# The first projection unit as eight plain block products, with the split of S3 behind 60 of its 96 matmuls

## The chip, the core and the metric

The kernel runs on one core of one Trainium2 chip. The metric is the device time of one execution in microseconds (us); the figure that is compared is the median of several executions.

## What is computed

One layer of a bidirectional encoder over 2048 tokens of width 1024. Only its first line matters here, the combined input projection:

```python
u = x @ w_in
idx = np.cumsum(SPLIT_SIZES)[:-1].tolist()
q, k, v, a_gate, hy, h_gate, br_gate = jnp.split(u, idx, axis=-1)
```

`x` is 2048 x 1024 and `w_in` 1024 x 8704. What follows (windowed attention, a long convolution by FFT, gates, the output projection and a layer norm) is not touched by the change.

## The kernel before

**Tiling.** The projection is made transposed: 128 output columns (one tile of `w_in`) stand on the partitions, 512 tokens along the free axis. A unit (class `Unit`, L209) makes two such column tiles for two token chunks, so four 128x512 results, from a 2x2 scheme of blocks: the 1024 long inner dimension is cut into two halves of four 128-row pieces (k = 0 to 3), the tokens into two chunks, the columns into two tiles. Instead of eight block products it uses seven, M1 to M7, by the scheme of Strassen and Winograd: M1 and M2 take the raw blocks A11 and A12 of x, the others take sums S1 to S4 of blocks or A22 (table `XOP`, L34), and on the side of the weights the blocks B11 to B22 or their sums T1 to T4 (`WOP`, `TDEF`).

**Split in two.** Every operand is split in a high and a low part of reduced width: `split` (L55) makes the high part by a cast on ScalarE (ACT) and the low part by a subtraction on VectorE (DVE) or GpSimd (POOL). A block product is then 4 pieces x 3 matmuls (high x high, high x low, low x high; L274, L276, L278) = 12 matmuls of 128x512, a unit 84.

**Weights.** `Unit.load` brings two tiles of 512 KB into `w_raw` (three buffers, shared by all units). `Unit.prep` makes, for one product, the weight's sum on DVE (`w_tmp`, L227) and its split, high part on ACT, low part `w_l` on POOL. It runs four products ahead, in a ring of five buffers.

**The order of products.** `stream` (L242) strings the units' products together: M1 of a unit, then (of the unit before it) M4 and M3, then M2, M6, M5, M7, and so on. It is a Python generator: each `next` of it writes down one matmul. `finish` (L283) empties the results: `keep` copies a PSUM bank to SBUF on ACT (L286), `add` joins two of them on DVE (L293), M4 is copied on ACT (L307). A unit's sums Y, X and Z take the banks y0 and y1 (changing places from unit to unit) and zz; bank c is not used in this stage.

**The start, `hy_stage(0)` (L349).** The first unit is a `z_unit` (L385), the second a `g_unit` (L429), and so on by turns, 16 units. For the first one x is not yet there: `load_x` brings the blocks of token chunk 0 (`r0[k]`, A11 and A12 side by side, 512 KB each) and of chunk 1 (`r1[k]`, A21 and A22). They are kept in buffers that later hold other things: `raw` (L358) uses the three `u` buffers and the two `cv` buffers, and two of the `r1` tiles use `w_raw`. `r1[2]` thus waits until `r0[0]` is done with, and `r1[3]` until a weight tile of the first unit is. Then `split_x` splits A11 and A12 (low parts on DVE) and `sums_x` (L165) makes for each k the sums S1 to S4 into `xs` tiles on DVE (L168) and splits S2, S1 (DVE), S3, A22 and S4 (POOL). A `u` buffer is needed again as soon as the first result of a unit leaves PSUM (`new_u`, L363).

**What sets the order.** The engines work each through a queue in order. The order in the queues is not the order of the text: a planner at build time (a list scheduler with its own timing, priority by the order of the text) sets it, and a buffer goes to its next owner when all accesses to the earlier one are done. So a transfer written down far later, as the copies of `w_branch_attn` to `wa_d` (L462, in the second pass), can stand near the start.

**Lines that matter below.** L56 and L57 are the two halves of `split`, L163 the loads of x, L219 those of the weights, L227 the sums of weights, L168 the sums of x, L286 and L307 copies out of PSUM, L366 a memset at the head of a fresh `u` buffer.

## Time and profile before

| | us |
|---|---|
| median of 3 executions | 2641.27 |
| lowest to highest | 2640.31 to 2643.61 |
| the profiled execution, time | 2640.98 |
| the profiled execution, span on the core | 2639.2 |
| TensorE matmul (PE) busy | 2505.1 (95% of the span) |
| DVE busy | 1735.0 (66%) |
| ACT busy | 1520.2 (58%) |
| POOL busy | 1406.8 (53%) |

The span is the time from the first to the last instruction on the core. Times in the rows below are counted from its start. "Busy" includes time in which an instruction has started and stands still. An engine's idle time is put down to what ended it (`<-` and the releaser).

### The profile page before, as it was taken

The page shows a single profiled execution, that of the slowest core. Times are in us where ns is not written, and L with a number is a line of the kernel's source. Part 1 is how long each engine was busy: PE and PEld are TensorE (multiplying, and loading weights), DVE is VectorE, ACT ScalarE, POOL GpSimd, SP SyncE. Part 2 cuts the span into 40 slices and gives each one's busy share as a digit, 9 for nine tenths or more (in the row PEclk, how much of TensorE's full clock was granted, in tenths as well). Part 3 has the DMA queues.
Part 4 walks back from the last instruction along what each step waited for, and adds up shares of the span by engine and source line. Part 5 has one row for each costly group of instructions (what it writes and reads, how often), then busy time and mean ns, then how long its engine had stood idle before and what let it go on. Part 6 is the DMA issues. An engine that isn't in the chain of part 4 may idle for free. (4 is left out here: it accounts for less than half of the span.)

```text
span 2639.2 us, 39177 instructions
## 1 busy us (share of the span) xinstructions
PE 2505.1 (95%) x12364; PEld 2088.9 (79%) x12364; DVE 1735.0 (66%) x3323; ACT 1520.2 (58%) x2935; POOL 1406.8 (53%) x1410
## 2 busy tenths in 40 slices
PE   6999999999999999999999999998989988999998
PEld 4888877786788877888887888886778866888887
DVE  7866677657577775655541577777989924556555
ACT  4444444468688864445455678887666644334432
POOL 6655554475666655665545666667766634112220
PEclk8999999999999999999999999999999998999999
DMA  7733343544544544245668545446777668556662
GB/s 255 235 120 122 120 155 119 167 150 146 180 144 150 156 160 139 81 136 179 198 190 261 165 137 157 126 141 226 244 242 252 214 200 221 136 130 168 176 154 78
DMA packets 342788, 444.04 MB, mean 168 GB/s; under 512 B 133257, under 2 KB 214619, under 8 KB 341029
## 3 DMA queue, kind: packets, MB, share of 16 engines
q1 hardware_dynamic: 340965, 432.50, 53.2%
q0 software_dynamic: 1616, 9.04, 1.1%
q8 instruction: 98, 1.61, 0.3%
q14 instruction: 109, 0.89, 0.1%
HBM read 290.41 MB, written 168.08 MB: 174 GB/s over the span
## 5 line engine op out<-in xcount | busy, mean ns | idle before, releaser
L57 POOL TENSOR_TENSOR w_l<-w_tmp,w_h 128x512 fp32r<-128x512 f32 x272 | 371.7, 1368 | 291.0 <-ACT w_h L56 254.5
L57 POOL TENSOR_TENSOR w_l<-w_raw,w_h 128x512 fp32r<-128x512 f32 x204 | 298.4, 1465 | 143.8 <-ACT w_h L56 118.8
L56 ACT CAST w_h<-w_tmp 128x512 fp32r<-128x512 f32 x272 | 168.1, 619 | 212.8 <-PE ps_y L276 167.2
L56 ACT CAST w_h<-w_raw 128x512 fp32r<-128x512 f32 x204 | 126.5, 621 | 146.2 <-PE ps_zz L276 74.5
L943 POOL TENSOR_TENSOR xq<-xq 128x512 fp32r<-128x512 f32 x128 | 162.9, 1297 | 83.0 <-ACT xq L941 79.9
L789 ACT ACTIVATE pb<-pb,rm 128x385 f32<-128x385 f32 (+1 forms) x256 | 153.3, 601 | 71.6 <-DVE rm L786 62.7
L380 DVE SCALAR_TENSOR_TENSOR cv<-u,cw,cv 128x1024 f32<-128x1024 f32 (+1 forms) x96 | 142.0, 1479 | 69.3 <-ACT cv L377 69.1
L274 PE MATMUL ps_y<-xq,w_h 128*128 128x512 f32 x376 | 150.1, 399 | 6.4 <-ACT u L286 6.3
L278 PE MATMUL ps_y<-xq,w_l 128*128 128x512 f32 x376 | 147.6, 392 | 0.0
L276 PE MATMUL ps_y<-xq,w_h 128*128 128x512 f32 x376 | 147.2, 391 | 0.0
L1236 POOL TENSOR_TENSOR ar<-ar,ga 128x256 f32<-128x256 f32 x64 | 51.1, 801 | 173.6 <-ACT ga L1235 156.1
L783 DVE CUSTOM_DVE_ANT_0 pb<-ps_a,bias 128x384 f32<-128x384 f32 (+1 forms) x256 | 131.2, 534 | 17.7 <-PE ps_a L53 12.2
L57 DVE TENSOR_TENSOR pl<-ps_b,ph 128x512 fp32r<-128x512 f32 (+1 forms) x240 | 130.1, 561 | 13.3 <-ACT ph L56 11.4
L227 DVE TENSOR_TENSOR w_tmp<-w_raw,w_tmp 128x512 f32<-128x512 f32 x94 | 89.6, 953 | 69.5 <-POOL w_l L57 68.5
L227 DVE TENSOR_TENSOR w_tmp<-w_raw 128x512 f32<-128x512 f32 x94 | 98.1, 1044 | 56.2 <-DMA w_raw<-in_w_in_dram 37.7
L57 POOL TENSOR_TENSOR fl<-fl,fh 128x512 fp32r<-128x512 f32 x32 | 43.2, 1349 | 166.7 <-ACT fh L56 166.5
L53 PE MATMUL ps_y<-yh,b 128*128 128x256 f32 x688 | 130.0, 283 | 0.0
L286 ACT COPY u<-ps_y 128x512 f32<-128x512 f32 x204 | 119.0, 583 | 6.2 <-PE ps_y L278 5.9
L53 PE MATMUL ps_y<-xq,w_h 128*128 128x512 f32 x336 | 113.2, 407 | 3.5 <-ACT u L286 3.5
L53 PEld LDWEIGHTS ps_y<-yh,b 128*128 128x128 f32 x688 | 109.7, 191 | 1.7
L293 DVE TENSOR_TENSOR ev<-ps_zz,u 128x512 f32<-128x512 f32 x72 | 49.4, 686 | 93.7 <-ACT u L286 34.4
L53 PE MATMUL ps_c<-pl,v 128*128 128x256 f32 x368 | 99.4, 296 | 11.3 <-DVE pl L57 10.8
(370 smaller groups left out, 8325.3 us busy)
## 6 DMA issues: line engine op xcount, KB each, us to landing
w_raw<-in_w_in_dram SPq DMA_DIRECT2D x136, 512.0 KB, 3.7
xq<-zk_d SPq DMA_DIRECT2D x64, 512.0 KB, 4.9
br_d<-ev SPq DMA_DIRECT2D x64, 256.0 KB, 2.0
zk_d<-ko SPq DMA_DIRECT2D x64, 256.0 KB, 2.0
zk_d<-zo SPq DMA_DIRECT2D x64, 256.0 KB, 4.1
gc_d<-go SPq DMA_DIRECT2D x64, 256.0 KB, 2.5
fl<-gc_d SPq DMA_DIRECT2D x64, 256.0 KB, 5.0
ga<-br_d SPq DMA_DIRECT2D x64, 256.0 KB, 3.6
```

The source lines that it names most:

```text
L53: tc.keep_in_program_order(nc.tensor.matmul(*args, **kw))
L56: nc.scalar.copy(out=hi, in_=src)
L57: return (eng or nc.vector).tensor_tensor(out=lo, in0=src, in1=hi.bitcast(F32), op=ALU.subtract)
L227: w_sum[0].tensor_tensor(out=self.tmp[n], in0=i0, in1=i1, op=ALU.subtract)
L274: mmf(o, wh[:, k], xh[k], start=start and k == 0, stop=False, skip_group_check=not start)
L276: mmf(o, wh[:, k], xl[k], start=False, stop=False, skip_group_check=not start)
L278: mmf(o, wl[:, k], xh[k], start=False, stop=k == 3, skip_group_check=not start)
L286: nc.scalar.copy(out=u.tmp[n], in_=o)
L380: nc.vector.scalar_tensor_tensor(out=y[:, i0:hi], in0=u[:, i0 + n:hi + n], scalar=cw[:, t, n:n + 1], in1=y[:, i0:hi], op0=ALU.mult, op1=AL ...
L783: nc.vector.tensor_tensor_reduce(out=pb[:, 0:W], in0=sc[:, 0:W], in1=bias[head][:, off:off + W], scale=1.0, scalar=-3.0e38, op0=ALU.add, o ...
L789: last_exp[0] = nc.scalar.activation(out=pb[:, 0:W + 1], in_=pb[:, 0:W + 1], func=AF.Exp, bias=rm[:, 1:2], accum_out=rm[:, 2:3])
L943: nc.gpsimd.tensor_tensor(out=l[:, i], in0=l[:, i].bitcast(F32), in1=h[:, i].bitcast(F32), op=ALU.subtract)
```

## The change

The first unit gets a flag `plain` and is made of eight block products P1 to P8 in place of M1 to M7. Each of the four results is the plain sum of two products that accumulate in a bank of their own (Y, X, Z and, for the fourth, bank c), and ACT copies it out; there are no sums of weights and no sums of x in it. P1 to P4 use A11 and A12, P5 to P8 use A21 and A22. The unit has 96 matmuls. A21 is a new split operand that shares its buffers with S4. The second unit follows with its seven products as before.

The loads of `r1[2]` and `r1[3]` go to four free tiles (two named `gate`, one `zh`, one `zl`) as four transfers of 256 KB. A21 and A22 are split ahead of the sums, A21 on DVE, A22 half on DVE and half on POOL. The sums S3 and S4 are written in place of their inputs, S3 over A21 in `r1`, S4 over A12 in `r0`. The split of S3 (POOL) is written down behind 60 of the 96 matmuls, that of S4 (POOL) behind all 96.

```diff
--- before.py
+++ after.py
@@ -36,6 +36,12 @@
 TDEF = dict(T1=("B12", "B11"), T2=("B22", "T1"), T3=("B22", "B12"), T4=("B21", "T2"))
 ACC = dict(M1=("Y", True), M2=("X", True), M3=("Z", False), M4=("Y", False), M5=("Z", True),
            M6=("Y", False), M7=("Y", False))
+PLAIN = dict(P1=("B11", "A11", "Y", 0), P2=("B21", "A12", "Y", 1), P3=("B12", "A11", "X", 0), P4=("B22", "A12", "X", 1),
+             P5=("B11", "A21", "Z", 0), P6=("B21", "A22", "Z", 1), P7=("B12", "A21", "W", 0), P8=("B22", "A22", "W", 1))
+PLAIN_OUT = dict(P2=(0, 0), P4=(1, 0), P6=(0, 1), P8=(1, 1))
+WOP.update({n: v[0] for n, v in PLAIN.items()})
+XOP.update({n: v[1] for n, v in PLAIN.items()})
+ACC.update({n: (v[2], v[3] == 0) for n, v in PLAIN.items()})
 ALPHA = 2.0 ** 0.25
 LN_EPS = 1e-5
 MAGIC = 12582912.0
@@ -152,6 +158,7 @@
                 parts = [big_tiles(n)] if n in BIGN else [(x_half(), x_half()) for _ in range(2)]
                 xparts[n] = parts
                 xops[n] = [[t[i][:, k] for t in parts for k in range(4 // len(parts))] for i in range(2)]
+            xops["A21"] = xops["S4"]
 
         def w_raw():
             return wpool.tile([P, KT, P], F32, name="w_raw", bufs=3)
@@ -163,19 +170,15 @@
             nc.sync.dma_start(out=dst, in_=a["xT"][:, 2 * p + c, k::4])
 
         def sums_x(k, r0, r1, tmp, engs):
-            def op(i0, i1, f=ALU.subtract):
-                o = tmp()
+            def op(o, i0, i1, f=ALU.subtract):
                 nc.vector.tensor_tensor(out=o, in0=i0, in1=i1, op=f)
                 return o
-            s1 = op(r1[:, 0], r1[:, 1], ALU.add)
-            s2 = op(s1, r0[:, 0])
+            s1 = op(tmp(), r1[0], r1[1], ALU.add)
+            s2 = op(tmp(), s1, r0[:, 0])
             split_x("S2", k, engs[0], s2)
             split_x("S1", k, engs[1], s1)
-            s3 = op(r0[:, 0], r1[:, 0])
-            split_x("S3", k, engs[2], s3)
-            s4 = op(r0[:, 1], s2)
-            split_x("A22", k, engs[3], r1[:, 1])
-            split_x("S4", k, engs[4], s4)
+            op(r1[0], r0[:, 0], r1[0])
+            op(r0[:, 1], r0[:, 1], s2)
 
         def split_x(n, k, e, src):
             h, l = xops[n]
@@ -211,6 +214,7 @@
                 self.t, self.dst, self.done = (t0, t1), dst, done
                 self.raw, self.ops, self.tmp = None, {}, {}
                 self.perm = False
+                self.plain = False
 
             def load(self):
                 if self.raw is None:
@@ -248,6 +252,9 @@
                     u.par = nunit[0] % 2
                     nunit[0] += 1
                     u.o = {}
+                    if u.plain:
+                        seq += [(u, m) for m in PLAIN]
+                        continue
                     seq.append((u, "M1"))
                 if prev:
                     seq += [(prev, "M4"), (prev, "M3")]
@@ -267,7 +274,7 @@
                     seq[i + look + 3][0].load()
                 b, start = ACC[m]
                 if start:
-                    u.o[b] = bank({"Y": ("y0", "y1"), "X": ("y1", "y0"), "Z": ("zz", "zz")}[b][u.par])
+                    u.o[b] = bank({"Y": ("y0", "y1"), "X": ("y1", "y0"), "Z": ("zz", "zz"), "W": ("c", "c")}[b][u.par])
                 o = u.o[b]
                 (xh, xl), (wh, wl) = xops[XOP[m]], u.ops.pop(m)
                 for k in range(4):
@@ -293,7 +300,13 @@
                 nc.vector.tensor_tensor(out=ts[0], in0=ts[1], in1=ts[2], op=ALU.add)
                 u.done(ti, c, d)
 
-            if m == "M1":
+            if m in PLAIN:
+                if m in PLAIN_OUT:
+                    ti, c = PLAIN_OUT[m]
+                    d = u.dst(ti, c)
+                    nc.scalar.copy(out=d, in_=o)
+                    u.done(ti, c, d)
+            elif m == "M1":
                 keep("u1")
             elif m == "M2":
                 add(0, 0, o, "u1")
@@ -469,6 +482,7 @@
                 g = stream(units, mm)
                 if p == 0:
                     alloc_x()
+                    units[0].plain = True
                     units[0].load()
                     next(g)
                     r0 = [raw(i) for i in range(4)]
@@ -479,15 +493,36 @@
                             split_x(n, k, nc.vector, r0[k][:, i])
                     r1 = []
                     for k in range(4):
-                        r1.append(raw(4 + k // 2) if k % 2 == 0 else
-                                  w_raw().rearrange("p a c -> p (a c)").rearrange("p (a c) -> p a c", a=2))
-                        load_x(0, 1, k, r1[k])
+                        if k < 2:
+                            r = raw(4) if k == 0 else \
+                                w_raw().rearrange("p a c -> p (a c)").rearrange("p (a c) -> p a c", a=2)
+                            load_x(0, 1, k, r)
+                            r1.append([r[:, 0], r[:, 1]])
+                            continue
+                        if k == 2:
+                            r1.append([hy.tile([P, CH], F32, name="gate", bufs=2) for _ in range(2)])
+                        else:
+                            r1.append([hy.tile([P, 4, P], F32R, name=n, bufs=2).bitcast(F32).rearrange(
+                                "p i c -> p (i c)") for n in ("zh", "zl")])
+                        for h in range(2):
+                            nc.sync.dma_start(out=r1[k][h], in_=a["xT"][:, 1, k + 4 * h])
                     nc.sync.dma_start(out=cw, in_=a["conv"])
                     consts()
                     for k in range(4):
+                        split_x("A21", k, nc.vector, r1[k][0])
+                        split_x("A22", k, (nc.vector, nc.gpsimd)[k % 2], r1[k][1])
+                    for k in range(4):
                         sums_x(k, r0[k], r1[k],
                                lambda: hy.tile([P, CH], F32, name="xs", bufs=7),
-                               (nc.vector, nc.vector, nc.gpsimd, nc.gpsimd, nc.gpsimd))
+                               (nc.vector, nc.vector, nc.gpsimd))
+                    for _ in range(60):
+                        next(g)
+                    for k in range(4):
+                        split_x("S3", k, nc.gpsimd, r1[k][0])
+                    for _ in range(36):
+                        next(g)
+                    for k in range(4):
+                        split_x("S4", k, nc.gpsimd, r0[k][:, 1])
                     run(g)
                 else:
                     for _ in range(9 * 84):
```

## Rows read from the trace of the kernel before

**Rows 1.** The page: PE's share, its busy tenths, its granted clock, in 40 slices.

```profile
PE 2505.1 (95%) x12364; PEld 2088.9 (79%) x12364; DVE 1735.0 (66%) x3323; ACT 1520.2 (58%) x2935; POOL 1406.8 (53%) x1410
...
PE   6999999999999999999999999998989988999998
...
PEclk8999999999999999999999999999999998999999
```

**Rows 2.** Windows: busy us of each engine (instructions), granted clock, DMA share, GB/s.

```profile
0.00:10.00 10.00, 0.90 (x2) 0.58 (x2) 4.02 (x5) 3.98 (x7) 3.25 (x7) 1.00 0.81 263
10.00:20.00 10.00, 8.40 (x24) 5.22 (x23) 8.93 (x13) 5.95 (x12) 5.05 (x3) 1.00 1.02 383
20.00:30.00 10.00, 4.16 (x11) 1.75 (x11) 6.00 (x10) 4.57 (x9) 9.29 (x4) 0.92 0.94 306
30.00:40.00 10.00, 5.99 (x12) 3.93 (x13) 8.70 (x8) 4.98 (x9) 8.51 (x10) 0.50 0.17 57
40.00:50.00 10.00, 6.14 (x15) 3.68 (x14) 8.98 (x6) 3.97 (x7) 9.39 (x8) 0.67 0.39 119
90.00:100.00 10.00, 10.00 (x45) 8.26 (x44) 8.44 (x8) 4.70 (x8) 7.14 (x9) 1.00 0.95 318
```

**Rows 3.** Timeline of PE: start, us, line, out<-in, shapes, [idle before <-releaser].

```profile
9.11 0.80 PE L274 MATMUL ps_y<-xA11h,w_h 128*128 128x512 f32 x1 [9.11 <-ACT xA11h L56]
...
49.84 0.63 PE L276 MATMUL ps_y<-xq,w_h 128*128 128x512 f32 x1
50.27 0.63 PE L278 MATMUL ps_y<-xq,w_l 128*128 128x512 f32 x1
...
62.40 0.39 PE L278 MATMUL ps_y<-xS2h,w_l 128*128 128x512 f32 x1
62.62 0.39 PE L274 MATMUL ps_y<-xA12h,w_h 128*128 128x512 f32 x1
...
75.83 0.50 PE L274 MATMUL ps_y<-xq,w_h 128*128 128x512 f32 x1 [1.15 <-ACT u L286]
```

**Rows 4.** Waits from 0 to 60 us: who for whom, us, times, longest.

```profile
PE ps_zz L274 <- ACT xS1h L56: 6.5, 1, 6.5
...
DVE xs L168 <- DMA u<-in_xT_dram: 5.3, 1, 5.3
```

**Rows 5.** Timeline of the DMA issues on SP's queue.

```profile
9.78 7.86 SPq L462 DMA_DIRECT2D wa_d<-in_w_branch_attn_dram  x8
18.23 0.38 SPq L163 DMA_DIRECT2D w_raw<-in_xT_dram  x1
21.25 0.38 SPq L163 DMA_DIRECT2D u<-in_xT_dram  x1
```

**Rows 6.** Timeline of DVE.

```profile
18.70 0.68 DVE L168 TENSOR_TENSOR xs<-xs,u 128x512 f32<-128x512 f32 x1
19.30 0.68 DVE L168 TENSOR_TENSOR xs<-u,cv 128x512 f32<-128x512 f32 x1
...
39.87 1.76 DVE L168 TENSOR_TENSOR xs<-xs,cv 128x512 f32<-128x512 f32 x1
41.56 1.77 DVE L168 TENSOR_TENSOR xs<-cv,w_raw 128x512 f32<-128x512 f32 x1
```

**Rows 7.** Timeline of POOL.

```profile
20.71 5.83 POOL L57 TENSOR_TENSOR xq<-xs,xq 128x512 fp32r<-128x512 f32 x1 [5.50 <-ACT xq L56]
26.50 1.25 POOL L57 TENSOR_TENSOR xq<-cv,xq 128x512 fp32r<-128x512 f32 x1
27.72 1.26 POOL L57 TENSOR_TENSOR xq<-w_raw,xq 128x512 fp32r<-128x512 f32 x1
```

**Rows 8.** One window: first POOL subtraction to the last of the sums; columns as above.

```profile
5.30:48.40 43.10, 24.67 (x60) 14.49 (x60) 36.05 (x38) 20.91 (x38) 33.57 (x25) 0.81 0.66 226
```

**Rows 9.** Timeline of ACT: a cast and a copy out of PSUM.

```profile
20.02 0.62 ACT L56 CAST xq<-xs 128x512 fp32r<-128x512 f32 x1
...
46.09 0.58 ACT L286 COPY u<-ps_y 128x512 f32<-128x512 f32 x1
```

## The prediction

> **What bounds the kernel now.** First the page: PE is busy 95% of the span, 9 or more tenths in nearly every slice but the first, where it has 6 at a granted clock of 0.8 [rows 1]. So time is saved where PE waits, and the largest such place is the start. Then the windows of 10 us: PE makes some 45 matmuls in a full window (90 to 100), but 24, 11, 12 and 15 in the four from 10 to 50, and its granted clock falls to 0.50, so to 1.2 GHz, between 30 and 40 [rows 2]. Third the timeline of PE: the first matmul starts at 9.11; the one at 62.62 is the first of the second unit's M2, and counted by product 108 lie before it, the first of them at 9.11 and the last at 62.40 [rows 3]. There they follow each other every 0.225 us (62.40 to 62.62), and later there is one hole of 1.15 us at 75.83, where a bank is not yet copied out [rows 3]. At that pace the 84 matmuls of one unit would end at 62.62 - 24 x 0.225 = **57.2 us**: of the first 57 us PE uses 84 x 0.225 = 19.
>
> Why it waits: the largest waits are PE for the high part of S1 (6.5 us), which waits for DVE, which waits 5.3 us for x [rows 4]. That x is late because `r1[3]` and `r1[2]` are issued at 18.23 and 21.25, when their buffers are free, behind eight 512 KB copies to `wa_d` [rows 5]. A second cause does not show among the waits. A DVE subtraction takes 0.68 us, one every 0.60, while POOL rests [rows 6]; a POOL subtraction takes 1.25, one every 1.22, while DVE rests [rows 7]. With both at work a DVE one takes 1.76 and the next starts 1.69 later [rows 6], close to 0.60 + 1.22 = 1.82. They take turns. Once POOL even stood 5.83 us on one subtraction while DVE worked on [rows 7]. The window 5.3 to 48.4 checks it: 38 DVE instructions and 19 POOL subtractions (25 less 5 memsets and one that begins at the edge) [rows 8]; 19 pairs x 1.69 + 19 single x 0.60 = 43.5 us, and the window has 43.1. So DVE and POOL together were **full from 5.3 to 48.4**, late x or not, and PE had made 60 matmuls by then [rows 8].
>
> The Trainium skill says the same in "SBUF — State Buffer", section "Who interferes with whom": the two engines share a port pair, held by one for a whole instruction. "Perfetto Trace Analysis", section "Optimizing Scalar/DVE Operations", turns that against changes like this: moving work between the two might not help. The 1.69 us agree with both.
>
> **The change, part by part.**
>
> *PE.* 96 matmuls for 84: 12 x 0.225 = 2.7 us more, contained in what follows, where the 96th is compared with the 84th of before.
>
> *Loads of x.* The four 256 KB issues go ahead of the `wa_d` copies and need no buffer to come free. Weights and x of the first unit are 5 MB; by 20 us before had moved 2.6 + 3.8 = 6.4 MB [rows 2], so they land by about 16.5 us. The wait of 5.3 us goes. The copies to `wa_d` come that much later; nobody needs them here. The issues cost 0.4 us each on SP [rows 5], hidden.
>
> *DVE and POOL.* Of DVE go four sums of weights and three joins, and A21 and half of A22 come: 6 subtractions. POOL loses two of A22 and gets one more weight (eight for seven). What P1 to P8 need is 8 weights and 2 of A22 on POOL, 8 + 6 on DVE: 10 x 1.69 + 4 x 0.60 = 19.3 us, done at 5.3 + 19.3 = 25 us if nothing else is put in front, some 4 us later with DVE's sums in between, since DVE has nothing better to do. PE can work on P1 to P4 from 9 us and on P5 to P8 as they come, so its 96th matmul ends about **33 us**.
>
> *The wait that the change adds.* P2's copy into a `u` buffer needs one of the three that hold `r0[0]` to `r0[2]`, and each is free only when S4's split of that k is done, since s4 stands there now. So the order is S4 split on POOL, memset, copy on ACT (0.58 [rows 9]), bank free. The first freed `u` buffer empties y0 and zz (P2, P6), the second y1 and c (P4, P8); M2 of the second unit needs y0, M1 needs y1. Before, M1's result went to a tile of its own. Queued behind the copy on ACT are the weights' casts of the second unit, and PE itself stands.
>
> *When is the second S4 split done?* On POOL 16 subtractions end with it: 8 weights, 2 of A22, 4 of S3, 2 of S4. On DVE nearly all 38 (8 + 6 + 24 for the sums) come first, since S3's last split needs the 23rd of the 24. So 16 x 1.69 + 22 x 0.60 = 40.2, from 5.3: **45.5 us**. Its lower bound: the planner may put S4's first two ahead of the last S3 and the sums of k = 2, 3; then POOL has 14 to 16 and DVE 26, 15 x 1.69 + 11 x 0.60 = 32 and the end is at 37. Its upper bound: three weights of the second unit stand ahead of it, 3 x 1.22 = 3.7 more, 49.2, but these are then ready. I take 45.5, since S3 is written first. M2 can start one pair earlier and M1 0.7 later, so I let PE go on at 45.5.
>
> *Clock and lag.* PE has stood some 12 us by then. Before, after such a stretch (granted clock 0.50 to 0.67 [rows 2]), matmuls came every 0.43 us (49.84 to 50.27 [rows 3]); seven at 0.43 for 0.225 cost 1.4 us. Weights of the second unit run closer to PE than before; POOL makes one in at most 1.7 us and PE uses one in 2.7, so I put 1 us for holes. The hole of 1.15 at 75.83 may go or stay; I count it as a gain, bounds 0 and 1.15.
>
> *ACT* gets four copies for four, five casts of 0.62 us more [rows 9]; it is busy 4 to 6 of 10 us [rows 2]: no cost while that cover holds, 3 us if not.
>
> *Sum.* 57.2 + 1.15 - 45.5 - 1.4 - 1.0 = **10.4 us** earlier, and all that follows is bound by PE and moves along. The profiled execution's 2640.98 becomes 2630.6; it lies 0.3 under the median, so I say 2631 for the median.
>
> **Rivals.**
>
> 1. *S4 comes early* (lower bound above): PE goes on at 37, the clock barely falls: 57.2 + 1.15 - 37 - 1 = 20, so **2621**. For it: S4 and S3 become ready at about the same time in the planner's eyes. Against: S3 stands first in the text. 0.15.
>
> 2. *POOL is kept out.* DVE's 24 sums follow each other without a gap and POOL stands, as in the 5.83 us row [rows 7]. From about 17 us, when DVE begins on them, 24 x 0.60 give 32 or 33 us before POOL goes on. It then has 18 subtractions left before the second unit can run (4 weights, 1 of A22, 8 of S3 and S4, 5 weights of the second unit), at the full 1.69 beside DVE's sums of weights and the first convolution: 33 + 30 = 63, and 57.2 + 1.15 - 63 - 1.4 = -6: **2647**, slower. It decides where POOL's last needed subtraction passes 57 us. Against: in 19 pairs of [rows 8] the turns were kept but for that one row, and with DVE done POOL takes 1.22: 33 + 22 = 55, a gain of 2. 0.12.
>
> 3. *No taking of turns.* If the sums cost PE nothing, the second unit starts at 34, and the gain is 57.2 + 1.15 - 34 = 24: **2617**. Against: 1.69 us a pair [rows 6]. 0.05. By the Trainium skill's "SBUF — State Buffer", section "Who interferes with whom", it cannot be, and the 1.69 agree.
>
> 4. *The planner undoes the 60.* It may move S3's split anywhere, as it moved the `wa_d` copies [rows 5]. With S3 first, P8's weight comes 4 x 1.69 = 7 us later, at some 36, and PE's 96th at 39, still ahead of 45.5: the same **2631**. 0.08.
>
> **How the numbers follow.** Forecast 0.60, rivals 0.15, 0.12, 0.05, 0.08. The range: from 2620 (rival 1, with a us for the hole) to 2641 (the forecast with the upper bounds 49.2 + 3 on ACT gives 2637, with rival 2's milder end 2639); it leaves out rival 3 and most of rival 2. What can be told from no change is 0.2%, 5.3 us, so faster means below 2636.0. Faster: 0.85 of the forecast and of rival 4, all of 1 and 3: 0.51 + 0.07 + 0.15 + 0.05 = 0.78. Slower: 0.09 of rival 2 and 0.02 of others: 0.11. The rest, 0.11, within.
>
> **What the next profile would show.** PE's first 96 matmuls without S1 or S2, the 96th at 30 to 39 us; all x loads issued before the `wa_d` copies; DVE and POOL taking turns at 1.7 us from about 15 us on; S4's splits ending at 42 to 49; a hole on PE of 8 to 14 us ahead of the second unit, ended by ACT's copies, with the clock down in it. The prediction is wrong if that hole is not there (rivals 1, 3), if PE stands for POOL's weights among P5 to P8 (rival 2), or if PE does not run full after 50 us.

## The result and the profile after

The changed kernel takes 2670.83 us in the median of 4 executions (2662.04 to 2676.66); the kernel before, beside it, 2640.79 (2640.25 to 2643.61). The ratio is 1.010, 95% interval 1.008 to 1.0119: **30 us slower** by the medians (21 to 31 by the interval), where 10 us faster was predicted, and outside the range. The profiled execution of after is the slowest of its four, 2676.66 with a span of 2674.9, so 5.8 us of the 35.7 by which the two profiled spans differ are not in the medians.

The page of after, in the parts shown of before in [rows 1] (PE's share, its busy tenths, its granted clock):

```profile
PE 2514.7 (94%) x12376; PEld 2098.3 (78%) x12376; DVE 1734.3 (65%) x3322; ACT 1518.7 (57%) x2940; POOL 1415.5 (53%) x1409
...
PE   6999989999899989999999999998889987999998
...
PEclk8999998999999999999999999999989989999999
```

The first slice has a 6 as before; 8s stand where before has 9s in the slices that begin at 334, 669, 936 and 1872 us, and a 7 for an 8 at 2207. So the head is not the only place, and the page alone doesn't say more. What does is one table, made from the timeline of PE: the start of the matmul before that has N ahead of it, and how much later or earlier the matmul with the same work still ahead of it starts in another kernel (in a kernel with the plain unit that one has N + 12 ahead of it). Negative is a lead. A row is one execution, the profiled one.

| N | 60 | 120 | 210 | 300 | 1000 | 1300 | 2800 | 5500 | 12300 |
|---|---|---|---|---|---|---|---|---|---|
| before, us | 49.2 | 65.3 | 86.4 | 106.8 | 261.9 | 328.1 | 702.6 | 1258.7 | 2616.2 |
| after, lag | -9.1 | -4.2 | -3.5 | +1.0 | +9.2 | +11.9 | +25.1 | +25.8 | +35.8 |

So the head did gain 9 us, half of which was gone 16 us later; **all of it was gone at 107 us, 11 us more were lost by 328, 13 more by 703, and 10 behind 1259.** Each of these is looked at by itself.

**The head.** Windows of 10 us of after, columns as in [rows 2]:

```profile
20.00:30.00 10.00, 5.25 (x24) 4.01 (x22) 10.00 (x18) 5.28 (x10) 10.00 (x1) 0.96 0.91 318
30.00:40.00 10.00, 4.62 (x12) 3.65 (x13) 3.06 (x5) 2.80 (x5) 10.00 (x7) 0.53 0.27 89
40.00:50.00 10.00, 7.03 (x30) 5.01 (x28) 6.16 (x5) 6.39 (x11) 10.00 (x13) 0.99 0.79 254
```

Between 20 and 30 POOL has one instruction in 10 us, DVE 18. The timeline of POOL shows it (answering [rows 7]), and that of DVE at its two ends (answering [rows 6]):

```profile
18.48 14.40 POOL L63 TENSOR_TENSOR xq<-w_raw,xq 128x512 fp32r<-128x512 f32 x1 [5.93 <-ACT xq L62]
32.85 2.48 POOL L63 TENSOR_TENSOR w_l<-w_raw,w_h 128x512 fp32r<-128x512 f32 x2
```

```profile
18.44 0.68 DVE L174 TENSOR_TENSOR xs<-w_raw 128x512 f32<-128x512 f32 x1
19.05 0.68 DVE L174 TENSOR_TENSOR cv<-u,cv 128x512 f32<-128x512 f32 x1
...
31.09 0.68 DVE L174 TENSOR_TENSOR zh<-cv,zh 128x512 f32<-128x512 f32 x1
```

One POOL subtraction, the low part of A22's second piece, stands for **14.40 us** while DVE starts one operation every 0.60 us, and ends 1.1 us behind DVE's last. Behind it in POOL's queue are two weights that PE needs. The waits of PE from 0 to 60 (who for whom, us, times, longest):

```profile
PE ps_c L285 <- POOL w_l L63: 10.1, 1, 10.1
PE ps_y L281 <- ACT xA11h L62: 8.7, 1, 8.7
PE ps_y L281 <- ACT w_h L62: 2.7, 1, 2.7
```

and the same on PE's timeline, with the last of the 96 matmuls between:

```profile
35.38 0.79 PE L285 MATMUL ps_c<-xq,w_l 128*128 128x512 f32 x1 [10.12 <-POOL w_l L63]
...
45.39 0.39 PE L285 MATMUL ps_c<-xq,w_l 128*128 128x512 f32 x1
48.47 0.50 PE L281 MATMUL ps_y<-xA11h,w_h 128*128 128x512 f32 x1 [2.69 <-ACT w_h L62]
```

What frees the banks are ACT's copies, the first two each right behind the S4 split that frees a `u` buffer (timeline of ACT), and the loads of x are issued ahead of `wa_d` (DMA issues on SP, answering [rows 5]):

```profile
42.47 0.59 ACT L307 COPY u<-ps_y 128x512 f32<-128x512 f32 x1 [2.75 <-POOL cv L388]
...
44.17 0.59 ACT L307 COPY u<-ps_y 128x512 f32<-128x512 f32 x1 [0.59 <-POOL xq L63]
...
47.32 0.58 ACT L307 COPY u<-ps_c 128x512 f32<-128x512 f32 x1
```

```profile
5.62 1.06 SPq L508 DMA_DIRECT2D gate<-in_xT_dram  x2
...
9.58 0.33 SPq L508 DMA_DIRECT2D zl<-in_xT_dram  x1
...
14.91 2.54 SPq L475 DMA_DIRECT2D wa_d<-in_w_branch_attn_dram  x4
```

**From 60 to 420 us.** The waits of PE before:

```profile
PE ps_y L274 <- ACT u L286: 2.9, 3, 1.2
PE ps_c L107 <- DVE ev L293: 1.3, 1, 1.3
```

and after:

```profile
PE ps_y L281 <- DVE u L300: 9.4, 7, 1.9
PE ps_c L113 <- DVE ev L300: 3.9, 1, 3.9
PE ps_zz L281 <- DVE gate L300: 3.0, 2, 1.5
```

4.2 us became 16.3 in these rows (in all rows of the two tables, 4.5 became 21.0). From 133 us on the waits for a join (L300) come every 40 us, which is two units; three of them on PE's timeline:

```profile
133.28 0.47 PE L281 MATMUL ps_y<-xA11h,w_h 128*128 128x512 f32 x1 [1.77 <-DVE u L300]
...
173.74 0.47 PE L281 MATMUL ps_y<-xA11h,w_h 128*128 128x512 f32 x1 [1.21 <-DVE u L300]
...
254.65 0.47 PE L281 MATMUL ps_y<-xA11h,w_h 128*128 128x512 f32 x1 [1.26 <-DVE u L300]
```

All are M1 of a unit (it runs on A11). The order of the products explains them. Read by operand from PE's queue, before runs every unit as M6, M2, M5, M7, then M1 of the next, M4, M3. In after every second unit has M1 of the next right behind M5, ahead of M7: M1 then needs its bank 12 matmuls earlier, and the join that empties it isn't done. Nothing in the diff touches these units; the planner found another order for them when their beginning changed. The order of the queues of the two kernels differs up to some 950 us, and behind that only in a few single swaps.

What this means for PE shows in the stretch from matmul 300 to 1300, before and then after (columns as in [rows 2]): PE has no idle time in it before and 9.0 us after.

```profile
106.80:328.10 221.30, 221.30 (x1002) 183.65 (x1001) 137.80 (x145) 103.86 (x164) 122.07 (x142) 1.00 0.39 122
107.80:340.00 232.20, 223.20 (x1002) 183.13 (x1001) 141.47 (x146) 101.08 (x165) 122.45 (x142) 1.00 0.37 117
```

**From 328 to 703 us** (340 to 728 in after). The same pair of rows from matmul 1300 to 2800:

```profile
328.10:702.60 374.50, 355.67 (x1501) 276.93 (x1500) 250.25 (x348) 212.14 (x378) 203.26 (x174) 0.99 0.46 153
340.00:727.70 387.70, 361.99 (x1501) 281.95 (x1500) 246.04 (x352) 211.01 (x381) 204.08 (x174) 0.96 0.45 149
```

Of the 13.2 us that after loses here, 6.9 are idle time of PE and 6.3 are longer busy time for the same matmuls, at a granted clock of 0.96 instead of 0.99: the lower of its two levels, 1.2 GHz, holds for 27 us of the stretch in after and for 10 before. A wait thus costs more than its own length. Behind the one of 5.1 us that ends at 702.52 (PE for ACT's copy of `ev`, L320), PE's matmuls start every 0.43 us, against 0.225 [rows 3].

### The profile page after: what moved, and what is told of

Same layout as the page of the kernel before. It is cut to its first block, busy times and chain, and to the rows that moved or that the text cites. A ratio compares the mean times of both kernels' runs of the same rounds, so it can differ in the third digit from the quotient of the medians.

```text
span 2674.9 us, 39181 instructions
## 1 busy us (share of the span) xinstructions
PE 2514.7 (94%) x12376; PEld 2098.3 (78%) x12376; DVE 1734.3 (65%) x3322; ACT 1518.7 (57%) x2940; POOL 1415.5 (53%) x1409
## 5 line engine op out<-in xcount | busy, mean ns | idle before, releaser
L281 PE MATMUL ps_y<-xq,w_h 128*128 128x512 f32 x368 | 145.8, 396 | 1.7 <-ACT u L293 1.5
L231 DVE TENSOR_TENSOR w_tmp<-w_raw 128x512 f32<-128x512 f32 x92 | 105.2, 1143 | 64.3 <-DMA w_raw<-in_w_in_dram 48.6
L283 PE MATMUL ps_y<-xq,w_h 128*128 128x512 f32 x368 | 144.0, 391 | 0.0
L231 DVE TENSOR_TENSOR w_tmp<-w_raw,w_tmp 128x512 f32<-128x512 f32 x92 | 78.2, 850 | 70.0 <-POOL w_l L63 69.1
L59 PE MATMUL ps_y<-xq,w_h 128*128 128x512 f32 x336 | 112.5, 404 | 3.2 <-ACT u L293 3.2
L300 DVE TENSOR_TENSOR ev<-ps_zz,u 128x512 f32<-128x512 f32 x72 | 49.4, 686 | 98.5 <-ACT u L293 43.5
```

Source lines behind the costliest of these rows:

```text
L59: tc.keep_in_program_order(nc.tensor.matmul(*args, **kw))
L231: w_sum[0].tensor_tensor(out=self.tmp[n], in0=i0, in1=i1, op=ALU.subtract)
L281: mmf(o, wh[:, k], xh[k], start=start and k == 0, stop=False, skip_group_check=not start)
L283: mmf(o, wh[:, k], xl[k], start=False, stop=False, skip_group_check=not start)
```

## The experiments

Theory after the first look: (1) POOL kept out by DVE makes the hole in the head; (2) the lead is given back by 107 us because DVE and POOL together are full until then; (3) the new order of later products costs the rest. Rival to (3): the early loads, or the position of the split of S3, or the head's delay itself carries on. All lags below are against the profiled execution of before, as in the table above; a ratio is against before's executions beside it.

### The early loads alone (e1_before_loads)

Before, with seven products as it was, and only the loads moved:

```diff
-                        load_x(0, 1, k, r1[k])
...
+                        if k == 2:
+                            r1.append([hy.tile([P, CH], F32, name="gate", bufs=2) for _ in range(2)])
+                        else:
+                            r1.append([hy.tile([P, 4, P], F32R, name=n, bufs=2).bitcast(F32).rearrange(
+                                "p i c -> p (i c)") for n in ("zh", "zl")])
+                        for h in range(2):
+                            nc.sync.dma_start(out=r1[k][h], in_=a["xT"][:, 1, k + 4 * h])
```

> The kernel before with only the early loads of x: r1[2] and r1[3] go to the four free tiles, the first unit keeps its seven products. Theory 1 (the loss lies in the order that the planner gives to the later units, and the plain unit brings it): VectorE's 5.3 us wait for x goes, the order of products from 100 us on stays as before, no wait of about 1.1 us for a join comes back every 40 us; 2634 to 2642 us. Rival (the early loads bring the loss, since they push the wa_d copies and all that the planner puts behind them): 2655 us or more.

Measured: 2647.17 us, ratio 1.0018 (1.0007 to 1.0029), 5 us above the theory's range and 8 below the rival's. The lag is -1.6 at matmul 210 and +1.8 at 300. The 5.3 us that DVE waited for x are gone and were worth nothing: the pair of DVE and POOL has the same work to do. In both kernels one of the two is busy at every moment from 5.3 to 48.4 us (idle together: 0.03 us before, none in e1). The order of products stays that of before, so the loads are not what brings the new one.

### The plain unit's weights on DVE (e2_after_wdve)

```diff
-                last_split[:] = [split(h, l, v, nc.gpsimd)]
+                last_split[:] = [split(h, l, v, nc.vector if m in PLAIN else nc.gpsimd)]
```

> The changed kernel with the low parts of the weights of P1 to P8 on VectorE instead of GpSimd. Theory 2 (GpSimd is kept out for 14.4 us by VectorE's gapless row of subtractions, and the weights of P6 to P8 wait behind it): PE's wait of 10.1 us for w_l goes, the 96th matmul ends at 33 to 37 us instead of about 48, the order of later products stays as in the changed kernel, total 6 to 12 us under it, 2659 to 2665 us. Rival (VectorE and GpSimd together are full, whoever is first): the hole only moves to the front of the second unit, PE has no more than 3 us gained at matmul 250, total within 3 us of the changed kernel.

Measured: 2657.95, ratio 1.007 (1.0055 to 1.0085), 3 thousandths better than after. Waits of PE, 0 to 60, of this kernel:

```profile
PE ps_zz L283 <- POOL xq L63: 7.3, 1, 7.3
PE ps_y L285 <- POOL w_l L63: 2.6, 2, 2.1
```

The wait for the weight is gone, and behind it stands the one for A22's own low part, which was still on POOL. The lead at 60 is 13.2 instead of 9.1, at 210 it is 7.8 instead of 3.5, and at 300 it is 1.9. At 1300 the kernel lags 8.1. The 96th matmul ends at 43.0, where the theory had 33 to 37.

### Another order written down (e3_after_m6first), and the same on before (e4_before_m6first)

The text of `stream` gives the order that before's planner found, M6 ahead of M2, in the first pass; the planner is still free.

```diff
-                    seq += [(prev, m) for m in ("M2", "M6", "M5", "M7")]
+                    seq += [(prev, m) for m in order]
...
-                g = stream(units, mm)
+                g = stream(units, mm, order=("M6", "M2", "M5", "M7") if p == 0 else ("M2", "M6", "M5", "M7"))
```

> The changed kernel with one change to the text's order of products in this stage, M6 ahead of M2, by which the planner comes back to the order of products that the kernel before has (M6, M2, M5, M7, M1 of the next, M4, M3). Theory 1 (order): the waits of 1.1 to 1.8 us for joins on VectorE every 40 us between 120 and 340 us vanish, the lag behind the kernel before at matmul 1000 falls from 9 us to between -4 and +2, total 2640 to 2660 us. Rival (backlog: VectorE and GpSimd are left behind by the start, so that joins come late in any order): the waits stay, the lag at matmul 1000 stays within 2 us of 9, total 2665 to 2675 us.

> Control: the kernel before with M6 ahead of M2 in the text's order, which leaves the order of products from the third unit on as it was. Theory 1: within 5 us of the kernel before, 2636 to 2646 us. Rival (the M6-first text is a gain or a loss by itself): outside of this.

Measured: on after 2650.55, ratio 1.0047 (1.0028 to 1.0065), so by the medians 20 us of the 30 came back by an order of lines alone; on before 2645.74, ratio 1.0021 (1.0009 to 1.0033), so the edit itself is no gain. The products of e3 stand in before's order, and its waits of PE from 60 to 420 are these:

```profile
PE ps_c L113 <- DVE ev L300: 3.6, 1, 3.6
PE ps_y L281 <- ACT u L293: 2.3, 2, 1.8
...
PE ps_y L281 <- DVE u L300: 0.2, 1, 0.2
```

The waits for a join went from 9.4 us to 0.2, and the lag from matmul 210 to 1300 from -0.7 to +0.2, where after goes from -3.5 to +11.9. That is (3), shown as far as matmul 1300. The hole of the head is still there (9.4 us for the weight): the two causes are separate.

### The split of S3 ahead of all 96 matmuls (e5_after_s3_first)

```diff
-                    for _ in range(60):
-                        next(g)
                     for k in range(4):
                         split_x("S3", k, nc.gpsimd, r1[k][0])
-                    for _ in range(36):
+                    for _ in range(96):
                         next(g)
```

> The changed kernel with S3's split written ahead of all 96 matmuls instead of behind 60. Theory (the planner undoes the place in the text): the queues of all engines hold the same instructions in the same order as in the changed kernel, the 14.4 us subtraction and the 10 us hole are there again, total within the spread of the changed kernel, 2662 to 2677 us. Rival (the place behind 60 matmuls keeps S3 out of the way of the weights of P5 to P8): three or four subtractions of S3 go ahead of these weights, the hole grows by 4 us or more, total 5 us or more above the changed kernel.

Measured: 2666.52, ratio 1.0093 (1.0074 to 1.0112), which after's interval overlaps. The order of all five engines' queues is that of after, instruction by instruction, and PE's wait for the weight is 9.8 us. Where the text puts the split is without any effect: the planner moves it to the same place.

### Both edits (e6_wdve_m6first)

The edits of e2 and e3 together.

> Both edits together: low parts of the weights of P1 to P8 on VectorE, and M6 ahead of M2 in the text. Theory 1 with 2 (the two losses are separate and add): the lead at matmul 210 stays at 7 to 9 us and is kept to matmul 1000, since no join makes PE wait every 40 us; total 2637 to 2646 us. Rival (what PE gains at the start it gives back while VectorE and GpSimd catch up, whatever the order): the lead at matmul 300 is under 2 us, total 2648 us or more.

Measured: 2650.28, ratio 1.0024 (1.001 to 1.0038). The lag is -12.3 at 60, -2.9 at 300 and -2.6 at 1300: once the sums are through, the lead that is left holds over 1000 matmuls. But the theory expected 7 to 9 us at 210 (measured 3.2) and 2637 to 2646 in all; the rival's 2648 or more came true, its lead under 2 us at 300 did not. Against e2 the order is worth 8.1 + 2.6 = 10.7 us at 1300; against after, e3 gave 11.9 - 0.2 = 11.7.

### The last four products without POOL (e7_after_no_pool)

With e3's order; the weights of P5 to P8 and all of A22 go to DVE.

```diff
-                last_split[:] = [split(h, l, v, nc.gpsimd)]
+                last_split[:] = [split(h, l, v, nc.vector if m in ("P5", "P6", "P7", "P8") else nc.gpsimd)]
...
-                        split_x("A22", k, (nc.vector, nc.gpsimd)[k % 2], r1[k][1])
+                        split_x("A22", k, nc.vector, r1[k][1])
```

> M6 ahead of M2, the low parts of the weights of P5 to P8 and all of A22 on VectorE, so that none of the first 96 matmuls waits for GpSimd once VectorE's row of subtractions begins. Theory 2: no wait of PE for GpSimd ahead of the 96th matmul, which ends at 32 to 36 us; the hole then stands in front of the second unit; lead at matmul 120 of 8 to 13 us, total 2634 to 2644 us. Rival (VectorE and GpSimd are full together): the 96th matmul is early but the second unit starts no earlier than in e6, and the lead at matmul 120 is within 2 us of e6's.

Measured: 2652.13, ratio 1.0042 (1.003 to 1.0054). POOL is kept out as before, now on a split of S3, that PE doesn't wait for (timeline of POOL, then waits of PE from 0 to 60):

```profile
22.73 14.00 POOL L63 TENSOR_TENSOR xq<-cv,xq 128x512 fp32r<-128x512 f32 x1 [11.75 <-ACT xq L62]
```

```profile
PE ps_y L281 <- ACT xA11h L62: 9.1, 1, 9.1
PE ps_y L281 <- ACT w_h L62: 8.8, 2, 7.6
```

The total misses the expected 2634 to 2644. Now the head looks as the prediction drew it: no wait for POOL's weights, a lead of 20.4 us at 60, and one hole of 7.6 us ahead of the second unit. But the lead is 9.8 at 120, 5.7 at 210 and 2.8 at 300, no more than in e6 which had 8 us less at 60. What was gained in the head is lost between matmul 60 and 300, the hole itself included.

### The second convolution's sums held back (e8_no_pool_late, e9_before_late, e10_wdve_late)

The sums of x for the next pair of token chunks (`sums_next`, on DVE, up to 100 us) are allowed only behind a multiplication on DVE (`z`) of the fourth to seventh pair of units. e8 does it to e7, e9 to before, e10 to e6.

```diff
-                            if 1 <= j <= 4:
-                                sums_next(j - 1)
+                            if 3 <= j <= 6:
+                                with tc.issue_after(zi.ins):
+                                    sums_next(j - 3)
```

> The kernel of e7 with the sums for the second half of x (27 VectorE subtractions and additions that ran between 43 and 99 us in the kernel before) held back until the fourth to seventh pair of units. Theory 3 (the lead of 20 us at matmul 60 is given back because VectorE and GpSimd together are full until about 100 us, whatever PE does): with 27 x 0.6 = 16 us less of their work before 100 us, the lead at matmul 300 is 8 to 14 us instead of 2.8 and stays to matmul 1000; total 5 to 11 us under e7, 2641 to 2647 us or less. Rival (the lead is lost by the order of joins and weights, not by the amount of work): the lead at matmul 300 is 1 to 5 us, total within 4 us of e7's 2652.

> The kernel before with the same 27 sums held back. Theory 3: VectorE and GpSimd are full in it too until 100 us, but there PE runs without a hole from 54 us on, so little is to be had: the lead at matmul 300 is 0 to 2 us, total 2636 to 2646 us. Rival (the later place of the sums is a gain by itself, so that e8 would say nothing of the plain unit): lead at matmul 300 of 4 us or more.

> The kernel of e6 with the same 27 sums held back. Theory 3: lead at matmul 300 of 7 to 11 us instead of 2.9, kept to matmul 1000; total 4 to 8 us under e6's 2650, so 2642 to 2646 us, level with the kernel before or a little over, since the re-planned stages from 400 to 700 us keep their loss. Rival: as in e8, a lead of 1 to 5 us and a total within 4 us of e6.

Measured: e8 2653.59, ratio 1.0039 (1.0026 to 1.0053); e9 2648.15, 1.0013 (0.9998 to 1.0028); e10 2650.14, 1.0025 (1.0013 to 1.0037). In the total nothing came of it: all three lie above what was expected. In the stage it did. Two windows of e7, then of e8, columns as in [rows 2]:

```profile
60.00:80.00 20.00, 16.14 (x68) 13.46 (x69) 16.52 (x19) 9.56 (x15) 11.28 (x12) 0.91 0.95 308
80.00:100.00 20.00, 17.98 (x77) 13.88 (x77) 17.71 (x20) 7.94 (x14) 13.91 (x13) 1.00 0.99 320
```

```profile
60.00:80.00 20.00, 18.72 (x80) 15.46 (x81) 11.99 (x16) 11.25 (x18) 10.31 (x13) 0.91 0.45 132
80.00:100.00 20.00, 20.00 (x90) 16.57 (x89) 11.23 (x12) 9.29 (x14) 11.90 (x15) 1.00 0.38 131
```

DVE falls from 34.2 to 23.2 of 40 us, and PE makes 170 matmuls for 145. From matmul 210 to 700 the lead stays 6.7 us to a tenth (e10: 5.9), where e7 went from 5.7 to 2.8 and e6 from 3.2 to 2.9. So the sums beside the second and third unit take 3 to 4 us of the lead at 300 (e10 against e6, e8 against e7): (2), shown, but smaller than thought, since leads of 8 to 14 (e8) and 7 to 11 us (e10) were expected. e9, which has a lag of 0.8 us there, says that their later place is no gain by itself. The larger fall, from 20.0 at 60 to 6.7 at 210, is there with the sums away: the hole of 7.6 us, PE's clock at 0.55 between 40 and 50, and 2.4 us for the convolution of the first unit (`cv`, L414). At 1000 matmuls e8's lead is 0.9: PE waits 5.4 us for joins again, with the products in before's order. e9 loses 4.5 us in the same stretch (0.8 at 700, 5.3 at 1300) and waits 4.6 for joins, so this comes with the sums in their new place.

### The order of the matmuls held fast (e11_before_fixed, e12_plain_fixed)

To take the planner's choice away, in both kernels all matmuls of the first pass's units are held to the order of the text (that of e3). e11 is before, e12 is e8; so the two differ not only in the plain unit but also in the sums held back.

```diff
-                g = stream(units, mm)
+                g = stream(units, mmo if p == 0 else mm, order=("M6", "M2", "M5", "M7") if p == 0 else ("M2", "M6", "M5", "M7"))
```

> Before, with the products of each unit of the first pass written in the order M6, M2, M5, M7 and TensorE's matmuls of that pass held to the order of the text, so that the planner can't move them. The base for the next run; on its own: theory (the planner's order of products is worth some 10 us in the first pass, and before had a good one by luck): within 0.3% of before, since this order has M1 of the next unit behind M7 as before's has. Rival (the order as such is worth nothing): the same, so this run decides only with the next.

> The changed kernel with the plain unit's weights of P5 to P8 and A22 on VectorE, the sums of the second convolution held back, and the same fixed order of matmuls in the first pass as in the run beside it. Theory (the head gains some 7 us net, and what eats it behind 190 us is the order of products that the planner finds anew): with the order fixed in both the lead of 6 to 7 us holds from 100 to 380 us, no PE waits for joins there, and the ratio to the run beside it is 0.997 to 0.999, unless the stages from 400 to 740 us are planned anew there and take 4 to 9 us. Rival (whatever its order, the head's lead is lost to later waits on VectorE and ScalarE, which don't move along): lag back to 0 or above by 380 us.

Measured: e11 2742.26, ratio 1.037 (1.0355 to 1.0385); e12 2737.7, ratio 1.0353 (1.0332 to 1.0375). That e11 would be within 0.3% of before was wrong by far. PE's waits from 60 to 380, e11 and then e12:

```profile
PE ps_b L107 <- DVE cv L401: 64.1, 7, 14.9
```

```profile
PE ps_b L113 <- DVE cv L414: 72.0, 7, 23.4
```

Each wait stands before the eight small matmuls that transpose a convolution's result: with the units' matmuls held, PE stands there until DVE has done the convolution, 9 to 10 us each time on average. As a base it is therefore poor: e11 lags before by 21.3 us at matmul 120 already and by 83.8 at 1300, e12 by 4.1 and 65.5, so the lead of e12 below is no measure of what the plain unit is worth. But the two have the same order on PE, and for that the pair does answer: the lead of e12 against e11 is 17.2 us at matmul 120, 17.2 at 210, 17.6 at 300, 18.2 at 1000 and 18.3 at 1300, that is from 69 to 394 us of e12. With one order of the matmuls on both sides a lead in the head moves along to the end of the first pass. Behind it 4.4 us are lost by matmul 2800 and another 6 to the end (7.9 left); the medians differ by 4.6 us with overlapping intervals.

### All lags side by side

| N | 60 | 120 | 210 | 300 | 1000 | 1300 | 2800 | 5500 | 12300 | ratio |
|---|---|---|---|---|---|---|---|---|---|---|
| after | -9.1 | -4.2 | -3.5 | +1.0 | +9.2 | +11.9 | +25.1 | +25.8 | +35.8 | 1.010 |
| e1 loads | +1.5 | -0.5 | -1.6 | +1.8 | +2.4 | +2.4 | +5.5 | +8.8 | +9.7 | 1.0018 |
| e2 weights on DVE | -13.2 | -7.9 | -7.8 | -1.9 | +5.2 | +8.1 | +12.7 | +16.0 | +17.9 | 1.007 |
| e3 order | -9.7 | 0.0 | -0.7 | -0.2 | +0.2 | +0.2 | +9.2 | +12.0 | +16.8 | 1.0047 |
| e4 before, order | +0.4 | +3.1 | +3.3 | +3.3 | +3.4 | +3.4 | +9.5 | +7.9 | +7.6 | 1.0021 |
| e5 S3 first | -9.0 | -5.4 | -2.2 | +1.9 | +10.0 | +12.8 | +24.1 | +22.9 | +27.0 | 1.0093 |
| e6 = e2 + e3 | -12.3 | -4.9 | -3.2 | -2.9 | -2.6 | -2.6 | -2.8 | +0.7 | +6.8 | 1.0024 |
| e7 | -20.4 | -9.8 | -5.7 | -2.8 | -2.8 | -2.8 | +9.9 | +7.3 | +15.5 | 1.0042 |
| e8 | -20.0 | -9.5 | -6.7 | -6.7 | -0.9 | +0.1 | +11.0 | +9.6 | +16.5 | 1.0039 |
| e9 before, late | -0.1 | +0.9 | +0.8 | +0.8 | +4.3 | +5.3 | +4.8 | +5.0 | +2.4 | 1.0013 |
| e10 | -13.1 | -6.1 | -5.9 | -5.9 | -3.5 | -2.3 | +4.4 | +3.9 | +5.7 | 1.0025 |

(e11 and e12 stand in the text above.) The lead in the first pass doesn't decide the ratio: **four of the kernels lead by 2 us or more at 300, and none of these is faster than before.** Between 1300 and 2800 (328 to 703 us) all but e6 and e9 lose 3 to 13 us. In e1, e3, e4, e6, e9 and e10 the queues of PE, DVE, ACT and POOL and the order of the DMA issues are those of before in this stretch, instruction by instruction, and these six lose 3.1, 9.0, 6.1, -0.2, -0.5 and 6.7 us. So a loss of up to 9 us comes here without another order. After, e2 and e5 share one other order, and they lose 13.2, 4.6 and 11.3.

## Why the prediction was wrong

**The step that failed** is the half sentence at the end of the sum: "all that follows is bound by PE and moves along". After leads by 9.1 us at matmul 60 and by 3.5 at 210, and lags by 11.9 at 1300: PE, without idle time from matmul 300 to 1300 before, stands for 9.0 us there in after. In the first pass the step holds where the order of the matmuls is the same on both sides (e11 and e12, 18 us kept from 69 to 394 us; e6, 2.9 to 2.6 us kept over 1000 matmuls). In the changed kernel it is not: a first unit that is ready at another moment got another order of the products behind it, and where before has 4.5 us of waits between 60 and 420, that order has 21.0. The prediction names the planner and lets it undo an edit, as rival 4, but has no term for what it does to the units that the diff leaves alone. By size:

- the new order of the products in the first pass: 11 to 12 us (e3 against after, e6 against e2, at matmul 1300). By the medians writing the order down was worth 21 us on after (30.0 over before against 9.1 in e3) and 10 on e2 (16.5 against 6.5 in e6), which takes in what it changes behind 328 us;
- from 328 to 703 us: 13 us in after, 11 in e5 and 5 in e2 with the same order there, -0.5 to 9 in six kernels with before's order. The order may have a part in it; no run shows one, and this loss is not to be put down to it. What is seen is that half of after's 13 is idle time of PE and half its lower clock;
- behind 1259 us: 10 us in the profiled execution of after, 4.1 in that of e5, whose queues are the same. So some 6 of the 10 are a difference between executions (that of after lies 5.8 us over its median); of the rest the cause stays open, as it does why e6, which leads by 2.6 us at 1300, is no faster than before.

Point by point, in the order of the prediction:

- *What bounds the head* was right: DVE and POOL as one resource, x late or not. e1 tested it alone, and 5.3 us less of waiting for x gave nothing. The count behind it was not: of the 19 POOL subtractions in [rows 8] only 12 took 1.58 to 1.82 us, as in a turn with DVE; five took 1.25 or 1.26, four of these beside a resting DVE from 26.50 on, and the others 1.41 and 5.83. The sum came out at 43.5 all the same, because a pair (1.69) costs about what its two singles do (1.82). And the reading stopped at 48.4 us. The windows of before from 60 to 100 have DVE at 37.5 of 40 us, so the pair has no slack to take up an earlier PE until about 100 us; e8 and e10 put 3 to 4 us on it.
- *Loads of x*: right, issued at 5.62 to 9.58, `wa_d` behind them at 14.91.
- *The 96th matmul at 33 us*: it ended at 45.8, since POOL was kept out. Where P5 to P8 need nothing of POOL (e8) it started at 34.42. So the assumption that failed is that the two take turns.
- *The second S4 split at 45.5, PE on at 45.5*: it ended at 44.14 and PE went on at 48.47, 3 us late, for the weights' casts queued on ACT behind the copies and the 1.25 us that the first convolution takes there. They were named as queued there and priced at nothing; with the upper bound of 49.2 the range covered it.
- *Clock and lag*: mis-sized in place. The hole came earlier (25 to 35 us) and the clock was down in it (0.53) and again from 50 to 60 us.
- *The gain of 10.4 us*: measured 9.1 at matmul 60, 4.2 at 120 and 3.5 at 210. In e8, whose first 96 matmuls run as forecast, 20.0, 9.5 and 6.7. So it was too high by 3.7 us even there, where the second unit started 3 us earlier than assumed: the 1 us for holes was too little, since PE then waits 2.4 for the first convolution, and runs longer at the lower clock (granted 0.55 from 40 to 50 us, 0.91 from 60 to 80). With the sums left where they are (e7) another 4 us go.
- *Rival 2, POOL kept out*: its mechanism is what happened in the head, to the microsecond: DVE's row at 0.60 until "32 or 33 us before POOL goes on", measured 32.85. Its price was wrong on the high side. It let PE go on at 63; DVE had nothing to do for 7 of the 10 us from 30 to 40, POOL worked off its backlog at 1.22 to 1.24 each until 39 us, and PE went on at 48.47, earlier even than by the milder price given beside it (55, a gain of 2; measured 3.5 to 4.2). The rejection, "in 19 pairs the turns were kept but for that one row", took a count for a rule, and the count was 12: that one row of 5.83 us was the case that the change makes, DVE with a long row of operations that wait for nothing. PE's 10.1 us for `w_l` in P7 are the sign that the prediction named for this rival. But with the hole gone (e7, 2652.13) the kernel is still no faster, so this is not the step that turned a gain into a loss.
- *Rival 4, the planner undoes the 60*: right, shown by e5 (identical queues). It was given 0.08 and had no effect on the time, as said.
- *Rivals 1 and 3*: not seen.

The Trainium skill ("SBUF — State Buffer", section "Who interferes with whom") has the engine that issues first hold the shared pair for a whole instruction. The trace goes beyond that in price: the subtraction of 18.48 stood while DVE started 21 instructions, not one. What the Trainium skill says of moving work between the two ("Perfetto Trace Analysis", section "Optimizing Scalar/DVE Operations", that it might not help) agrees with e7 and e6, which move different splits from POOL to DVE and lead by 20.4 and 12.3 us at matmul 60, but by 2.8 and 2.9 at 300.

## What to carry to other kernels

Where a planner orders the queues, a change at the head is priced in two parts, what the stage gains and what the new order of everything behind it costs; the second can be the larger (11 us of order against 9 of head here), and a control with the order written down, on both kernels, separates them. Before a later loss is put down to another order, compare the queues: six kernels with one and the same order in a stretch of 375 us differed by up to 9.5 us in it. Two engines that share a resource are to be added up as one to the end of the stretch where that sum is full, not to the end of the stage that one edits: part of a lead is given back for as long as the sum is full (3 to 4 us here). When one row of a trace contradicts an average (5.83 us against 12 turns of about 1.69), ask what made that row and whether the change makes more of it.

## What was not expected of the hardware

- POOL can be kept from one subtraction, 1.25 us when alone, for 14.40 us (after), 14.00 (e7), 13.99 (e8) and 16.80 (e2), for as long as DVE starts an operation with two operands in SBUF every 0.60 us. In other stretches the two take turns at 1.69 [rows 6]. In each of these four cases the POOL instruction ended 1.1 us behind the end of the row on DVE. What decides which of the two patterns comes was not tested.
- Executions of after spread over 14.6 us in four runs, those of before over 3.4 in the four beside them, but over 14.4 in 22 others. No run here explains it, and lags of single executions behind 328 us are to be read with it.
- Holding PE's matmuls to one plausible order cost 3.7% (e11), 64.1 us of it in seven waits for the transposes behind a convolution.
